# First feed-forward product of a hybrid encoder layer: one of four weight sums a pair added by the transfer from DRAM, and the low part of one weight block formed by a rounding transfer within SBUF

## The chip, the cores and the metric

The kernel runs on one core of one Trainium2 chip. The metric is device time in microseconds (us) for one execution of the whole layer; lower is better. Of the kernel before, three runs were timed, and one more execution was recorded by the hardware profiler. An engine is named as in the profile: PE multiplies matrices, PEld loads its weights, DVE and ACT are the vector and scalar engines, POOL is GpSimd, SP issues DMA transfers.

## The reference

One layer of an encoder on 1024 tokens of width 1024: two attention groups, a cross-attention into 256 memory tokens, and a feed-forward block of hidden width 4096, each with a norm before and after. The part that matters here is the last one:

```python
h = rmsnorm(x, g_ff_pre[l])
y = jnp.square(jax.nn.relu(h @ w_ff1[l])) @ w_ff2[l]
x = x + rmsnorm(y, g_ff_post[l])
```

All values are float32.

## The kernel before, in words

**Numbers in two parts.** A float32 operand of a product is split into a high part (the value rounded to the type fp32r, by a copy on ACT) and a low part (the value less its high part, on DVE or POOL). `mm3` (lines 172 to 176) multiplies high by high, high by low and low by high: three matmuls of 128x128 by 128x512.

**The first feed-forward product.** `w_ff1` is cut into 32 column blocks of 128 columns, each loaded as one tile of 128 partitions by 1024 (512 KB). They are taken in 16 pairs (block j and block j + 16), and the tokens in two halves, so that one pair is a 2x2 block product. It is done in Strassen's way with seven products instead of eight, each of 12 matmuls: with the left half of the weights' features called k0 and the right half k1, a pair needs the block sums that `Weights.sums` and `Weights.sum4` (lines 1799 to 1811) make from the two raw tiles r0 and r1:

- line 1802: sc[k1] = r0[k0] - r1[k0]
- line 1803: r1[k0] = r1[k0] + r1[k1], in place, so that r1 becomes the block "s1a"
- line 1804: sc[k0] = r1[k0] - r0[k0]; sc is the block "s23"
- line 1809: sd = r0[k1] - sc[k0], the block "s4"

Each is a 128x512 operation. Pair 0 has them on DVE, ahead of the loop (`cur.sums(nc.vector)`), and pairs 1 to 15 on POOL. `Weights.split` (lines 1813 to 1820) then splits the blocks: high part on ACT (line 1597), low part on DVE (line 1600).

**The loop over pairs.** Instructions are written out by hand, and each engine runs its own in that order. In the pass of pair j stand, in this order: the sums of pair j + 1; the load of r0 of pair j + 2; from pair 7 on the two products with block "a" (`first_row`; for pairs 0 to 6 these were made before the loop and kept in DRAM, and `reload` brings them back as tile p1r, line 1841); the product of s23 with T2 into bank x; u2 = x + p1 (line 1943); the stores of the pair before (`sums()`); the product of s1a with T1 into bank z; the splits of "a" (from pair 7 on) and s23 of pair j + 1; the product of s23 with T3, added into bank x, so that it waits for the reading of x at line 1943; u3 (line 1958 on DVE for pairs 0 to 6, line 1960 on ACT after that) and g22 = z + u3 (line 1962); the load of r1 of pair j + 2; the reload of p1r of pair j + 1; the product of s1a with T4 into bank v; the split of s1a of pair j + 1; the product of s4 with B22, added into bank z, so that it waits for line 1962. So a pass is five products for pairs 0 to 6 and seven for pairs 7 to 15.

**Buffers.** Raw weight tiles rotate through three buffers of tag wraw; only r1 of pair 1 (`wfu`, line 1794) is taken from the pool u4. High and low parts of "a" and "s1a" rotate through two buffers each. The pool u4 (lines 153 to 155) holds tiles of 4 KB a partition for the whole kernel: tokens in two parts, queries and keys, some weights, x, p1r. A tile gets a buffer at its first write, and that write waits until an earlier tile of the buffer has been used for the last time. All transfers are issued by SP, in order.

**The plan of the attention phase.** From line 459 on, a planner in Python orders the instructions of the attention phase with costs and tokens; it counts six free u4 buffers at its start and gives and takes such tokens. `Outputs.pump` (lines 878 to 886) starts the first group of output loads (lines 920 to 929) once 12 tokens are free.

**Scratch for descriptors.** Line 2184 builds the program with a scratch space of 256 bytes a partition for transfers that POOL issues; the kernel before issues none.

Of the kernel before, what the change touches and what calls it, by code (L numbers as in the profile page):

```python
# [17 lines left out]
AF = mybir.ActivationFunctionType  # L18
ALU = mybir.AluOpType
# [116 lines left out]
def build(ctx, tc, nc, out, t):  # L136
    def pool(name, bufs=1, space=None, stack=ctx, **kw):
        if space is not None:
            kw["space"] = space
        return stack.enter_context(tc.tile_pool(name=name, bufs=bufs, reuse_waits="tile", **kw))  # L140
# [4 lines left out]
    up = pool("u4")  # L145
# [6 lines left out]

    def u4(name, shape, dt=F32R):

        return up.tile(list(shape), dt, tag="u4", bufs=34, name=name)

    class Act:


        def __init__(self, name, n=HT):  # L160
            self.per = 1024 // n
            m = KC // self.per
            self.h = [u4(f"{name}_hi{i}", (P, self.per, n)) for i in range(m)]
            self.l = [u4(f"{name}_lo{i}", (P, self.per, n)) for i in range(m)]
# [35 lines left out]
    od = [[[dr.tile([P, HT], F32, name=f"od{k}_{h}{m}") for m in "hl"] for h in range(2)] for k in range(KC)]  # L200
# [18 lines left out]
    def bias_rows(part):  # L219

        if part == 0:
# [13 lines left out]
    free = {k: Tokens(flow, n) for k, n in  # L235
            dict(s=2, tr=2, pv=2, mm=2, sp=5, p=2, klo=4, bias=2, raw=2, w=2, ot=3, u4=6,
                 q=4, mp=4, pt=1, xt=2, wq=0).items()}
    seen = {}

    def there(*keys):  # L240
        return all(flow.past(seen.get(k, math.inf)) for k in keys)
# [11 lines left out]
    class Stock:  # L253
# [48 lines left out]
        def hi(self, key):  # L302
            raw, nm = self.raw[key], "_".join(map(str, key))
            home, shape = self.home.get(key, "w"), list(raw.shape)
            if home == "w":
                w = [wp.tile(shape, F32R, tag=x, bufs=2, name=x + nm) for x in ("whi", "wlo")]
            elif home == "wq":
                w = [p2x.tile(shape, F32R, tag="wq", bufs=2, name=x + nm) for x in ("whi", "wlo")]
            else:
                w = [u4(x + nm, shape) for x in ("whi", "wlo")]  # L310
            nc.scalar.activation(w[0], raw, AF.Copy)
            self.w[key] = w
# [243 lines left out]
    def turn_steps():  # L556
        for n, a, g in units:
            for c, (kbs, slots, dead) in enumerate(key_steps(n, g)):
                yield (0.109 * (4 - len(dead)),
                       lambda: there(("p", n, a, g, 0), ("p", n, a, g, 1)) and free["tr"].ready() and free["p"].ready())  # L560
                free["tr"].take()
                free["p"].take()
                nm = f"{n}{a}{g}{c}"
                live = slice(1 if dead == [0] else 0, 3 if dead == [3] else 4)
                whole = mark(("t", n, a, g, c))
                tr = mm_tile([P, 4, P], f"ptr{nm}", "tr")
                ph = p1.tile([P, 4, P], F32R, tag="ph", bufs=2, name=f"ph{nm}")
                pl = p1.tile([P, 4, P], F32R, tag="pl", bufs=2, name=f"pl{nm}")
                for m, (j, q) in enumerate(slots):
                    if m not in dead:  # L570
                        sp, b0, i = probs[n, a, g][q]
                        k = kbs[j] - b0
                        nc.tensor.transpose(tr[:, m, :], sp[:, k * P:(k + 1) * P], ident)  # L573

                def split(at, ph=ph, pl=pl, tr=tr, live=live, whole=whole):
                    def done(end):
                        whole(end)
                        free["tr"].give(end)
                    flow.put("V", at, 0.56 if dead else 0.7, lambda: nc.vector.tensor_sub(pl[:, live, :], tr[:, live, :],  # L579
                                                                        f(ph[:, live, :])), done)  # L580

                flow.put("S", flow.end, 0.49 if dead else 0.6, lambda ph=ph, tr=tr, live=live: nc.scalar.activation(  # L582
                    ph[:, live, :], tr[:, live, :], AF.Copy), split)
                trs[n, a, g, c] = ph, pl
            for _ in range(1 + (g > 1)):
                free["sp"].give(flow.end)
# [285 lines left out]
    class Outputs:  # L872
# [5 lines left out]
        def pump(self):  # L878
            while self.left:
                th, g = self.left[0]  # L880
                if not (there(("od", g)) and ((th, g) == (0, 0) or there("keys")) and free["u4"].ready(12 if (th, g) == (0, 0) else 9)):
                    break
                self.left.pop(0)
                for _ in range(9):
                    free["u4"].take()
                self.one(th, g)

        def one(self, th, g):
# [21 lines left out]
            for i in range(2):  # L910
                for j in range(2):
                    kc = g * 4 + i * 2 + j
                    gc, o, dh, dl = gcol[:, kc:kc + 1], os[i][:, j, :], yh[i][:, j, :], yl[i][:, j, :]
                    dst = sq if kc % 4 == 0 else o

                    low = ol[i][:, j, :]

                    def loaded(at, gc=gc, o=o, dh=dh, dl=dl, dst=dst, low=low, last=i == 1 and j == 1):
                        flow.chain(at, [
                            (eng, add_cost, lambda: adder.tensor_add(o, o, low)),  # L920
                            ("S", 0.63, lambda: nc.scalar.activation(dh, o, AF.Copy, scale=gc)),
                            ("V", 0.75, lambda: nc.vector.scalar_tensor_tensor(
                                dl, o, gc, f(dh), op0=ALU.mult, op1=ALU.subtract))],
                            lambda end: (split(end), flow.put("S", end, 0.63, lambda: nc.scalar.activation(
                                dst, o, AF.Square), squared, 1)), 1)

                    here = all_of(("oin", th, kc), 2, loaded)
                    for m, x in enumerate((o, low)):
                        flow.load(flow.now, lambda x=x, kc=kc, m=m: nc.sync.dma_start(x, od[kc][th][m]), here, 3.0)
# [619 lines left out]
    NP = FF // (2 * P)  # L1549
# [117 lines left out]
    class Turn:  # L1667
# [26 lines left out]
        def sums(self):  # L1694
            a, i = self.a, self.i
            b12, b22 = self.src
            c12, d2 = t2(f"c12_{a}{i}"), t2(f"T2_{a}{i}")
            nc.scalar.activation(c12, b12, AF.Copy)
            d1, d4 = xf[i, a], xf[i + 2, a]
            nc.vector.tensor_sub(d1, b12, d1)  # L1700
            lo22 = self.hi("B22", b22)
            nc.vector.tensor_sub(d2, b22, d1)
            lo2 = self.hi("T2", d2)
            nc.vector.tensor_sub(c12, b22, c12)
            lo1 = self.hi("T1", d1)
            lo22()
            nc.vector.tensor_sub(d4, d2, d4)
            lo3 = self.hi("T3", c12)
            lo4 = self.hi("T4", d4)
            self.los = [lo2, lo1, lo3, lo4]  # L1710
# [71 lines left out]
    k0, k1 = slice(0, HT), slice(HT, D)  # L1782

    class Weights:
# [14 lines left out]
        def sums(self, eng=nc.gpsimd):  # L1799
            j, (r0, r1) = self.j, (self.raw[0], self.raw[1])  # L1800
            sc = pw.tile([P, D], F32, tag="sc", bufs=1, name=f"sc{j}")
            eng.tensor_sub(sc[:, k1], r0[:, k0], r1[:, k0])  # L1802
            eng.tensor_add(r1[:, k0], r1[:, k0], r1[:, k1])
            eng.tensor_sub(sc[:, k0], r1[:, k0], r0[:, k0])
            self.src = {"a": (r0, D, wp, "w"), "s23": (sc, D, pws, "v"), "s1a": (r1, D, wp, "w")}

# [5 lines left out]
        def split(self, n):  # L1812
            raw, width, p, tag = self.src[n]
            if p is pws:
                q = self.j % 2
                self.w[n] = HiLo(raw, width, pws[q], f"{tag}{q}", 1, f"{n}{self.j}").both(nc.vector)
            else:
                self.w[n] = HiLo(raw, width, p, tag, 2, f"{n}{self.j}").both(nc.vector)

    cur, nxt = Weights(0), Weights(1)  # L1820
    cur.load(0)
# [99 lines left out]
    with manual:  # L1921
        sums = lambda: None
        for j in range(NP):
# [20 lines left out]
            else:  # L1944
                nc.scalar.activation(u2, x, AF.Copy)
            sums()
            relu2(g11)
            put(j, 0, g11)
# [50 lines left out]

            cur, nxt = nxt, after  # L2000
        sums()


# [184 lines left out]
```

## Time and profile before

| what | value |
|---|---|
| median of three runs | 1492.26 us (1491.24 to 1492.3) |
| the profiled execution's own time | 1491.91 us |
| its span, first to last instruction | 1490.1 us |
| PE busy | 1466.0 us, 98% |
| DVE, ACT, POOL busy | 928.4, 795.2, 375.7 us |
| loop over pairs 0 to 15 | about 909 to 1170 us of the span |
| granted TensorE clock | 0.997 |

The span leaves out 1.81 us around the instructions. Busy time of PE counts matmuls that overlap, so a share near 100% says that PE had something in it, not that it ran at its peak. A line number in the profile is that of the kernel's text; where a helper issues an instruction (1597, 1600, 174 to 176), the tile's name tells which block it is.

### The profile page before, as it was taken

To read this page: it belongs to the slowest core of one execution; us is meant where nothing else is said; L and a number is where in the kernel's file an instruction comes from. 1 tells how busy PE (TensorE), PEld (TensorE's weight loads), DVE (VectorE), ACT (ScalarE), POOL (GpSimd) and SP (SyncE) were. 2 spreads that over 40 slices of the span, in tenths; PEclk is the share of its full clock that TensorE was granted. 3 is DMA by queue.
4 is the path that set the end of the run, shared out by engine and by line. 5 is a ranking of instruction groups with operands and counts; after the bars stand their busy time and mean duration, and the time that the engine had idled before them with its cause. 6 is when DMAs were issued, how large, how long until landed. Compare 5 with 4: busy or idle time off the path is not lost. (4 is left out here: it accounts for less than half of the span.)

```text
span 1490.1 us, 21429 instructions
## 1 busy us (share of the span) xinstructions
PE 1466.0 (98%) x7564; PEld 1249.1 (84%) x7564; DVE 928.4 (62%) x1599; ACT 795.2 (53%) x1426; POOL 375.7 (25%) x464
## 2 busy tenths in 40 slices
PE   8899999999999999999999999999999999999998
PEld 7788888888889987888888887888888888888886
DVE  4857666566465654884374587675555665646577
ACT  6647666666566663554363455555555553443442
POOL 1324354344343310431031423432333000000021
PEclk9999999999999999999999999999999999999999
DMA  8033323524225568461251355764445685436475
GB/s 326 29 87 107 86 67 79 168 79 133 77 75 155 175 234 313 156 212 57 85 170 57 126 171 201 265 233 155 149 157 175 234 344 191 141 129 209 173 252 198
DMA packets 95355, 239.54 MB, mean 161 GB/s; under 512 B 11896, under 2 KB 20224, under 8 KB 95248
## 3 DMA queue, kind: packets, MB, share of 16 engines
q1 hardware_dynamic: 95248, 238.18, 47.8%
q8 instruction: 59, 0.97, 0.3%
q14 instruction: 48, 0.39, 0.1%
HBM read 170.45 MB, written 59.30 MB: 154 GB/s over the span
## 5 line engine op out<-in xcount | busy, mean ns | idle before, releaser
L579 DVE TENSOR_TENSOR pl<-ptr,ph 128x512 fp32r<-128x512 f32 (+1 forms) x152 | 92.3, 616 | 63.2 <-ACT ph L582 62.6
L582 ACT ACTIVATE ph<-ptr 128x512 fp32r<-128x512 f32 (+1 forms) x152 | 79.6, 539 | 48.7 <-PE ptr L573 45.4
L1912 ACT ACTIVATE whif<-ra 128x1024 fp32r<-128x1024 f32 x37 | 39.2, 1060 | 122.6 <-PE fy L175 62.6
L1914 DVE TENSOR_TENSOR wlof<-ra,whif 128x1024 fp32r<-128x1024 f32 x37 | 45.3, 1225 | 91.4 <-ACT whif L1912 91.3
L2028 POOL TENSOR_SCALAR rf<-sf 128x1 f32<-128x1 f32 x8 | 7.4, 928 | 326.4 <-ACT jf L2013 326.1
L174 PE MATMUL fx<-vhif,whif 128*128 128x512 f32 x168 | 65.4, 390 | 0.0
L176 PE MATMUL fx<-vhif,wlof 128*128 128x512 f32 x168 | 65.4, 389 | 0.0
L175 PE MATMUL fx<-vlof,whif 128*128 128x512 f32 x168 | 65.4, 389 | 0.0
L613 PE MATMUL pv<-pl,vs 128*128 128x256 f32 (+1 forms) x304 | 64.6, 294 | 0.2 <-DVE pl L579 0.2
L613 PEld LDWEIGHTS pv<-ph,vs 128*128 128x128 f32 x304 | 53.2, 189 | 7.3
L613 PE MATMUL pv<-ph,vs 128*128 128x256 f32 (+1 forms) x304 | 58.1, 273 | 0.0
L1802 POOL TENSOR_TENSOR sc<-wf,wf 128x512 f32<-128x512 f32 x14 | 21.2, 1513 | 142.3 <-DMA wf<-in_w_ff 121.3
L174 PE MATMUL k<-hT_hi,whik 128*128 128x512 f32 x128 | 52.9, 413 | 0.0
L174 PE MATMUL mq<-h2T_hi,whimq 128*128 128x512 f32 x128 | 51.7, 404 | 0.0
L174 PE MATMUL yw<-whiwo,yT_hi 128*128 128x512 f32 x128 | 50.9, 398 | 0.7 <-ACT yt L1065 0.7
L174 PE MATMUL q<-hT_hi,whiq 128*128 128x512 f32 x128 | 51.0, 398 | 0.0
L175 PE MATMUL k<-hT_lo,whik 128*128 128x512 f32 x128 | 50.5, 395 | 0.0
L174 PE MATMUL ym<-whimo,oT_hi 128*128 128x512 f32 x128 | 50.4, 395 | 0.1
L176 PE MATMUL k<-hT_hi,wlok 128*128 128x512 f32 x128 | 50.4, 394 | 0.0
L175 PE MATMUL q<-hT_lo,whiq 128*128 128x512 f32 x128 | 50.2, 392 | 0.0
L175 PE MATMUL mq<-h2T_lo,whimq 128*128 128x512 f32 x128 | 50.1, 391 | 0.0
L176 PE MATMUL q<-hT_hi,wloq 128*128 128x512 f32 x128 | 50.1, 391 | 0.0
(597 smaller groups left out, 4989.4 us busy)
## 6 DMA issues: line engine op xcount, KB each, us to landing
ra<-gd SPq DMA_DIRECT2D x56, 512.0 KB, 3.9
wg<-in_w_ff SPq DMA_DIRECT2D x56, 512.0 KB, 5.1
wf<-in_w_ff SPq DMA_DIRECT2D x38, 512.0 KB, 3.8
gd<-s SPq DMA_DIRECT2D x48, 256.0 KB, 2.1
wrawmq<-in_w_mq SPq DMA_DIRECT2D x16, 512.0 KB, 4.1
wrawmo<-in_w_mo SPq DMA_DIRECT2D x16, 512.0 KB, 3.8
gd<-u SPq DMA_DIRECT2D x32, 256.0 KB, 2.1
gd<-g SPq DMA_DIRECT2D x25, 256.0 KB, 2.9
```

The lines of the kernel that those rows point to most:

```text
L174: nc.tensor.matmul(ps, lh, rh, start=start, stop=False, skip_group_check=more)
L175: nc.tensor.matmul(ps, lh, rl, start=False, stop=False, skip_group_check=more)
L176: nc.tensor.matmul(ps, ll, rh, start=False, stop=stop, skip_group_check=more)
L579: flow.put("V", at, 0.56 if dead else 0.7, lambda: nc.vector.tensor_sub(pl[:, live, :], tr[:, live, :], f(ph[:, live, :])), done)
L582: flow.put("S", flow.end, 0.49 if dead else 0.6, lambda ph=ph, tr=tr, live=live: nc.scalar.activation(ph[:, live, :], tr[:, live, :], AF.C ...
L613: nc.tensor.matmul(pv[:, q0:q0 + k1 - k0, :], v, x[:, k0:k1, :], start=c == 0 and m == 0, stop=c + 1 == len(steps) and m == 3, skip_group_ ...
L1802: eng.tensor_sub(sc[:, k1], r0[:, k0], r1[:, k0])
L1912: nc.scalar.activation(ah, ra, AF.Copy)
L1914: nc.vector.tensor_sub(al, ra, f(ah))
L2028: nc.gpsimd.tensor_scalar(r, ssf[b][:, 0:1], ssf[b][:, 1:2], EPS, op0=ALU.add, op1=ALU.add)
```

## The change

Four things are changed.

1. In `sums`, line 1803 is no longer an addition. POOL issues a transfer that reads the right half of block j + 16 from DRAM a second time and adds it to r1[k0] in SBUF. That holds for all 16 pairs, pair 0 among them, whose other sums stay on DVE.
2. In `split`, the low part of s1a of pairs 1 to 15 is no longer a subtraction on DVE. ACT writes the negated block, rounded to fp32r, into the low tile; then POOL issues a transfer within SBUF that adds the raw block to it.
3. The program is built with the default scratch space for descriptors in place of 256 bytes, and the pool u4 has 30 buffers in place of 34.
4. The first group of output loads in the attention phase starts at 11 free tokens in place of 12. The planner's count of free buffers at its start stays at six.

```diff
-        return up.tile(list(shape), dt, tag="u4", bufs=34, name=name)
+        return up.tile(list(shape), dt, tag="u4", bufs=30, name=name)
...
-                if not (there(("od", g)) and ((th, g) == (0, 0) or there("keys")) and free["u4"].ready(12 if (th, g) == (0, 0) else 9)):
+                if not (there(("od", g)) and ((th, g) == (0, 0) or there("keys")) and free["u4"].ready(11 if (th, g) == (0, 0) else 9)):
...
             eng.tensor_sub(sc[:, k1], r0[:, k0], r1[:, k0])
-            eng.tensor_add(r1[:, k0], r1[:, k0], r1[:, k1])
+            nc.gpsimd.dma_start(r1[:, k0], t['w_ff1'][j + NP].rearrange('p a b -> p (a b)')[:, k1], accum_op=ALU.add)
             eng.tensor_sub(sc[:, k0], r1[:, k0], r0[:, k0])
...
-                self.w[n] = HiLo(raw, width, p, tag, 2, f"{n}{self.j}").both(nc.vector)
+                h = self.w[n] = HiLo(raw, width, p, tag, 2, f"{n}{self.j}")
+                if n == "s1a" and self.j:
+                    h.split_hi()
+                    nc.scalar.activation(h.lo, raw, AF.Copy, scale=-1.0)
+                    nc.gpsimd.dma_start(h.lo, raw, accum_op=ALU.add)
+                else:
+                    h.both(nc.vector)
...
-    nc = bacc.Bacc("TRN2", target_bir_lowering=False, num_devices=1, dynamic_dma_scratch_size=256)
+    nc = bacc.Bacc("TRN2", target_bir_lowering=False, num_devices=1)
```

## The prediction

> **What bounds the kernel now.** I read the page's first part for the span, then busy time in windows, and last the timelines, engine by engine, around the places that the change touches.
>
> ```profile
> span 1490.1 us, 21429 instructions
> PE 1466.0 (98%) x7564; PEld 1249.1 (84%) x7564; DVE 928.4 (62%) x1599; ACT 795.2 (53%) x1426; POOL 375.7 (25%) x464
> ```
>
> ```profile
> 325.00:350.00 25.00, 25.00 (x156) 22.26 (x155) 11.44 (x31) 13.90 (x29) 8.32 (x10) 1.00 0.40 129
> ...
> 475.00:600.00 125.00, 123.37 (x696) 107.10 (x695) 74.90 (x147) 72.50 (x133) 24.89 (x27) 1.00 0.68 232
> ...
> 900.00:907.00 7.00, 6.33 (x28) 4.92 (x27) 5.25 (x9) 3.72 (x6) 0.00 (x0) 1.00 0.32 85
> 907.00:921.00 14.00, 12.97 (x58) 10.33 (x56) 8.95 (x12) 5.11 (x7) 5.15 (x4) 1.00 0.98 342
> ...
> 948.00:962.00 14.00, 14.00 (x63) 11.61 (x62) 10.08 (x13) 7.76 (x13) 5.18 (x4) 1.00 0.76 262
> 1003.00:1100.00 97.00, 97.00 (x430) 80.34 (x429) 50.13 (x61) 51.70 (x78) 29.26 (x21) 1.00 0.44 149
> ```
>
> A row of the windows has the stretch and its length, then busy us of PE, PEld, DVE, ACT and POOL, the granted clock, the share of the transfer engines' time and GB/s. In the two rows from 948 to 1100 PE is busy in every microsecond, while DVE, which the change relieves, has 50.13 of 97 and POOL 29.26: taking work from either shortens nothing there. PE's idle time in the loop lies in 907 to 921: 14.00 less 12.97, 1.0 us. That is all there is to gain in the loop; the question is which new waits reach PE.
>
> **The two durations that no row shows.** X is the time from a POOL-issued adding transfer of 256 KB from DRAM to its landing, Y that of the 512 KB transfer within SBUF. The nearest rows (KB each, median us from issue to landing):
>
> ```profile
> wf<-in_w_ff SPq DMA_DIRECT2D x38, 512.0 KB, 3.8
> gd<-s SPq DMA_DIRECT2D x48, 256.0 KB, 2.1
> x<-in_x SPq DMA_DIRECT2D x8, 512.0 KB, 9.7
> x1d<-xtw SPq DMA_DIRECT2D x8, 512.0 KB, 2.6
> p1r<-p1d SPq DMA_DIRECT2D x7, 512.0 KB, 5.6
> ```
>
> X lies between 2.1 (a plain store) and 9.7 (the crowded start), Y between 2.6 and 9.7. An adding transfer must read its target too and passes through POOL, so I take more than a plain load: X = 4 where the transfer engines are a third busy (before 907), 5 for both X and Y where they are full. The Trainium skill (DMA: Bandwidth & Descriptors, Anatomy of one DMA, SWDGE path) fits 2.0 us plus bytes over 436 GB/s for a transfer that POOL issues; by it, as an estimate, X is 2.6 and Y 3.2, the terms below come to 4.7 us in place of 10.4, and no row here can show it, since the kernel before has no such transfer.
>
> **Pair 0's sums (change 1).** These are ahead of the loop on DVE:
>
> ```profile
> 904.38 0.69 DVE L1803 TENSOR_TENSOR wf<-wf 128x512 f32<-128x512 f32 x1
> 905.11 0.69 DVE L1804 TENSOR_TENSOR sc<-wf,wf 128x512 f32<-128x512 f32 x1
> ...
> 906.93 1.23 DVE L1600 TENSOR_TENSOR v0lo_s<-sc,v0hi_s 128x1024 fp32r<-128x1024 f32 x1 [0.40 <-ACT v0hi_s L1597]
> ...
> 909.38 0.39 PE L176 MATMUL px<-T_hi,v0lo_s 128*128 128x512 f32 x1
> ...
> 914.81 0.69 DVE L1943 TENSOR_TENSOR u<-px,p1r 128x512 f32<-128x512 f32 x1 [1.92 <-DMA p1r<-p1d]
> ...
> 915.56 0.50 PE L174 MATMUL px<-T_hi,v0hi_s 128*128 128x512 f32 x1 [1.03 <-DVE u L1943]
> ```
>
> (A row of a timeline has start and length in us, engine and line, the tiles written and read, and in brackets the idle time before it with what ended it.)
>
> Line 1803 starts at 904.38, when line 1802 is done. In its place the transfer is issued, and line 1804 waits on DVE for its landing: 904.4 + 4 = 908.4 in place of 905.11. Queued behind it on DVE are sd, the low part of s23 and the low parts of T1 and T3; ACT waits for sc. Line 1804 ends at 909.1, the high part (1.06 for 128x1024, as in the next fence) at 910.2, the low part (1.23) at 911.4. PE's first low product of the loop starts at 909.38 in the trace, so it comes 2.1 late. The 1.03 us that PE then waited at 915.56 for u2, and u2 for p1r, is swallowed by that, so the product with T3 of pair 0 starts 1.1 late. The removed addition gives back 0.69 and costs 4.
>
> **Pairs 0 and 1 (changes 1, 2 and 3).**
>
> ```profile
> 914.83 1.28 POOL L1803 TENSOR_TENSOR wfu<-wfu 128x512 f32<-128x512 f32 x1
> ...
> 917.50 1.06 ACT L1597 ACTIVATE v1hi_s<-sc 128x1024 fp32r<-128x1024 f32 x1 [1.47 <-POOL sc L1804]
> ...
> 918.60 1.33 DVE L1600 TENSOR_TENSOR v1lo_s<-sc,v1hi_s 128x1024 fp32r<-128x1024 f32 x1 [3.09 <-ACT v1hi_s L1597]
> 919.85 0.68 DVE L1958 TENSOR_TENSOR u<-px,p1r 128x512 f32<-128x512 f32 x1
> 920.56 0.69 DVE L1962 TENSOR_TENSOR g<-pz,u 128x512 f32<-128x512 f32 x1
> ...
> 921.40 0.47 PE L174 MATMUL pz<-B_hi,u0hi_s 128*128 128x512 f32 x1
> ...
> 916.91 0.46 SPq L1841 DMA_DIRECT2D p1r<-p1d  x1
> ...
> 929.65 0.39 PE L174 MATMUL px<-T_hi,v1hi_s 128*128 128x512 f32 x1
> ```
>
> These rows are one chain already: POOL's third sum, ACT, DVE, and behind DVE's split, in order, u3 and g22, for which PE's B22 product waits. With the transfer the third sum runs from 914.8 + 5 = 919.8 to 921.1; high part to 922.1, low part to 923.4, u3 to 924.1, g22 to 924.8, and B22 starts at 924.9 in place of 921.4: 3.5 late.
>
> Then the buffers. When `reload` brings p1r of pair 1, the pool u4 holds 28 tiles of the tokens (8 for B11 and B21, 20 for the five blocks T1 to T4 and B22), `wfu`, p1r of pair 0 and this one: 31. With 34 buffers SP issued it at 916.91; with 30 it waits for the last use of `wfu`, which is now the rounding transfer of s1a of pair 1. ACT reaches that block at 922.1 (high part to 923.2, negated copy to 924.2), and with Y = 5 it lands at 929.2. SP issues the reload at 929.3, 5.6 more to 934.9, u2 0.7, and PE's T3 product of pair 1 starts at 935.7 in place of 929.65: **6.1 late** in all, the 3.5 and 1.1 within it. Stores of g22 and u3 and the next r0 stand behind the reload on SP; their readers come later than that. T1 of pair 1 needs the low part only at 930.9.
>
> **Pairs 2 to 6.** Rows of pair 2:
>
> ```profile
> 946.92 0.69 DVE L1962 TENSOR_TENSOR g<-pz,u 128x512 f32<-128x512 f32 x1
> ...
> 948.69 0.39 PE L174 MATMUL pz<-B_hi,u0hi_s 128*128 128x512 f32 x1
> ...
> 950.38 1.29 POOL L1802 TENSOR_TENSOR sc<-wf,wf 128x512 f32<-128x512 f32 x1 [7.12 <-DVE u1lo_s L1600]
> ```
>
> g22 ends at 947.61, 1.1 ahead of B22. A cycle closes here: first sum 2.8 after g22 (950.38), 1.3, X, third sum 1.3, then 3.7 for ACT's high part, DVE's low part, u3 and g22: 9.1 + X against a pass of 13.6. It decides at X = 4.5; at X = 5 each of five passes loses 0.5, less the 1.1 of slack: 1.4. The low part of s1a follows the third sum by 3.2 (ACT's two high parts and the negated copy) + Y, and PE reads it 9.6 after that sum (3.7, then B22 and T2 of 2.7 each, and 0.5): covered up to Y = 6.4. POOL waits for the negated copy with the next pair's first sum behind it, but that sum comes 6.5 after the third, later than the copy. **1.4**.
>
> **Pairs 7 to 15.** A pass is 19 us, and the covers are long:
>
> ```profile
> 1061.94 1.72 POOL L1802 TENSOR_TENSOR sc<-wf,wf 128x512 f32<-128x512 f32 x1 [12.88 <-DMA wf<-in_w_ff]
> ...
> 1060.18 1.06 ACT L1597 ACTIVATE whi_s1a<-wf 128x1024 fp32r<-128x1024 f32 x1 [1.89 <-PE pv L175]
> 1075.11 1.04 ACT L1597 ACTIVATE v1hi_s<-sc 128x1024 fp32r<-128x1024 f32 x1
> ...
> 1071.54 0.39 PE L176 MATMUL pz<-T_hi,wlo_s1a 128*128 128x512 f32 x1
> ...
> 1064.87 0.38 SPq L1585 DMA_DIRECT2D wf<-in_w_ff  x1
> ...
> 1073.82 0.32 SPq L1621 DMA_DIRECT2D gd<-s  x1
> ```
>
> The third sum must be done by 1075.1; from 1061.9 that leaves 10.6 us for X less POOL's wait for ACT's negated copy. That copy ends at 1062.2 and the low part is read at 1071.5, so Y may take 9.2. ACT's extra 1.05 falls into its idle time. The raw buffer is held until the landing, past 1064.87 where SP refilled it before; SP's next transfer stands at 1073.82. **0**, and beyond 9 us the wait is PE's.
>
> **The early buffers (change 3).** At the first projections u4 holds 16 tiles of tokens, 8 of values, 4 of weights and 2 of queries: 30. The two key tiles make 32.
>
> ```profile
> 79.89 1.21 ACT L709 ACTIVATE kd<-k 64x512 fp32r<-64x512 f32 x2 [3.40 <-PE k L176]
> ...
> 81.13 1.41 DVE L710 TENSOR_TENSOR kl<-k,kd 64x512 fp32r<-64x512 f32 x2 [1.08 <-ACT kd L709]
> ...
> 84.91 0.39 PE L176 MATMUL q<-hT_hi,wloq 128*128 128x512 f32 x1
> 85.13 0.39 PE L174 MATMUL k<-hT_hi,whik 128*128 128x512 f32 x1
> ```
>
> ACT's write of the keys must wait for a buffer, the first to come free being the query weights, last read at 84.91 + 0.39. Then 1.2 on ACT and 1.4 on DVE, to 88.0, before PE may write the same PSUM bank (two of that tag, and the other is just filled). PE started at 85.13: **2.9**. SP's copies of the keys and the bias loads behind them move by 5 us, and the first scores by 2.9 with PE.
>
> **Change 4** starts a group of loads and adds earlier at about 342 us, where PE is busy 25.00 of 25.00. Without a row of that order I take 0, between -2 (the stretch 475 to 600 has 125.00 less 123.37, 1.6 us, of idle PE) and +5 (four POOL additions of 1.3 in front of POOL's softmax work).
>
> **Sum.** 6.1 + 1.4 + 2.9 = 10.4. The span 1490.1 becomes 1500.5, the profiled execution 1491.91 (1.81 outside the span) 1502.3; the median of the runs, 1492.26, is 0.35 above that execution: **1502.7**.
>
> **Rivals.** *The transfers are slower, or the transfer engines fill up.* In 948 to 962 they are 0.76 busy at 262 GB/s, so full at 345. A pair adds 0.79 MB: 2.3 us of their time if moved once, 4.6 if the target is read as well, and 3.3 of 13.6 are free. The second count would overflow by 1.3 us a pass, and loads, reloads and stores would be late together. The Trainium skill (DMA: Bandwidth & Descriptors, Queues, rings and completion order) has each transfer engine take turns packet by packet between queues, so that a queue of POOL's own would bring no engines of its own; the share of 0.98 in pair 0 is where it would show first. With X = Y = 7: pairs 0 and 1 lose 10.0 by the same chain (the reload at 933.3), five passes 2.5 for X and 0.6 for the low part, less 1.1: 2.9 + 10.0 + 14.4 = 27, **1519**. It decides from X = 4.5 on.
>
> *No slower.* The buffers decide: if the framework finds the key tiles and p1r buffers whose last use is over, 2.9 and the reload's wait fall away, and only B22's wait in pair 0 stays, X - 1.5; below X = 4.5 that is under 3 us: **1493 to 1495**. Against it speaks the count of live tiles.
>
> *Faster.* Change 4 alone can do it, by filling PE's gaps after 475; it would have to bring over 6 us, and the gaps of that stretch are 1.6.
>
> *The forecast with quick transfers*, X = 2.6 and Y = 3.2: **1497**.
>
> **How the numbers follow.** Forecast with its quick variant, 1496 to 1509: 0.57. Slower transfers, 1509 to 1530: 0.28. No slower: 0.12. Faster: 0.03. A measurement tells 0.2% (3 us) from no change, so slower by more holds 0.85, within 0.12, faster 0.03. The range runs from 1494 to 1522: it leaves out the faster case, about half of the one with no change and the upper quarter of the slow one, some 0.16.
>
> **What would show it.** ACT's first key write at about 85.4; the reload of pair 1 on SP at about 929; g22 and B22 of pair 0 at 925; POOL's third sum 5 us after its transfer's issue; PE full from pair 7 on. Wrong would be PE stalls in pairs 7 to 15 (X or Y beyond 9), or a pass of pairs 2 to 6 well over 13.6.

## The result and the profile after

The changed kernel takes 1515.39 us in the median of four runs (1509.43, 1513.63, 1517.14, 1517.68), beside 1491.76 for the kernel before, timed with it: 1.0157 times as long, with a 95% interval of 1.0141 to 1.0173, so 23.6 us slower. The profiled execution is the quickest of the four (1509.43), so its trace shows 17.6 us of the 23.6 in its span.

First the page after the change: span and busy time, the transfer queues, the issues.

```profile
span 1507.7 us, 21486 instructions
...
PE 1469.6 (97%) x7564; PEld 1248.3 (83%) x7564; DVE 912.7 (61%) x1583; ACT 809.3 (54%) x1441; POOL 380.9 (25%) x480
...
q1 hardware_dynamic: 95248, 238.18, 46.2%
q0 software_dynamic: 4464, 12.06, 4.4%
...
wf<-in_w_ff SPq DMA_DIRECT2D x38, 512.0 KB, 4.7
gd<-s SPq DMA_DIRECT2D x48, 256.0 KB, 2.9
...
wlo_s1a<-wf POOLq DMA_DIRECT2D x14, 512.0 KB, 4.7
```

DVE is 16 us less busy, as the change meant it to be, and that shortens nothing. Queue q0 is new: 12.06 MB that keep all 16 transfer engines for 4.4% of 1507.7, 66 us. SP's queue moves 238.18 MB in 46.2%, 697 us. POOL's queue takes 5.5 us a MB, SP's 2.9. Loads of 512 KB land after 4.7 us in place of 3.8.

Next, what PE waits for from 900 us to 1200 us after the change (total, times, longest):

```profile
PE px L174 <- ACT v0hi_s L1597: 5.4, 1, 5.4
PE pz L176 <- DMA wlo_s1a<-wf: 5.3, 4, 1.6
PE pz L174 <- DVE g L1968: 1.3, 3, 0.7
PE px L174 <- DVE u L1949: 1.1, 1, 1.1
PE px L176 <- DVE wlo_a L1600: 0.8, 1, 0.8
```

Three of these are new: the high part of s23 of pair 0 (the run-in), four low parts of s1a (the rounding transfer), and g22. The fourth, u2 behind the reload, has moved from pair 0 to pair 1. They come to 13.1 us, 1.0 of which was there before, while the kernel falls 17.8 us behind from the start of the loop to its end (table below). Much of the rest is the clock, as the windows show (PE, PEld, DVE, ACT, POOL busy, granted clock, transfer share, GB/s; a packet counts in the window in which it starts, so a share can pass 1):

```profile
82.90:87.00 4.10, 4.06 (x11) 3.23 (x12) 1.30 (x2) 0.00 (x0) 0.00 (x0) 0.61 0.88 202
...
908.00:913.00 5.00, 0.49 (x3) 0.07 (x1) 0.95 (x2) 0.26 (x1) 0.00 (x0) 1.00 1.03 303
913.00:920.00 7.00, 6.11 (x14) 4.33 (x15) 6.60 (x8) 3.90 (x6) 2.55 (x2) 0.52 0.32 82
942.00:1010.00 68.00, 62.98 (x272) 50.18 (x270) 34.94 (x49) 38.80 (x58) 25.68 (x23) 1.00 0.95 280
1020.00:1187.00 167.00, 166.51 (x734) 137.17 (x733) 76.30 (x94) 94.22 (x141) 46.91 (x41) 1.00 0.64 186
```

From 913 to 920 PE is busy, but with 14 matmuls in 7 us, at a granted clock of 0.52. From 942 to 1010 (most of pairs 2 to 6) PE lacks 5.0 of 68 us, and the transfer engines are at 0.95. From pair 7 on PE is all but full: 166.51 of 167 us.

Matching PE's matmuls one by one between the two timelines gives the balance:

| matmul | before | after | later by |
|---|---|---|---|
| a key product just ahead of the new wait | 75.05 | 70.14 | -4.9 |
| first product of the second key tile | 85.13 | 82.94 | -2.2 |
| scores, some 15 us on | 100.13 | 99.81 | -0.3 |
| last products ahead of the loop | 900.22 | 899.49 | -0.7 |
| T2 of pair 0, first matmul | 908.93 | 913.85 | +4.9 |
| T3 of pair 0 | 915.56 | 922.56 | +7.0 |
| T3 of pair 1 | 929.65 | 937.43 | +7.8 |
| T1 of pair 2, first low part | 940.98 | 950.72 | +9.7 |
| the same of pair 5 | 981.78 | 996.00 | +14.2 |
| the same of pair 6 | 995.38 | 1011.26 | +15.9 |
| in pair 7 | 1025.07 | 1041.17 | +16.1 |
| second product, fx | 1200.09 | 1217.21 | +17.1 |

This execution began 4.9 us ahead by chance (the same product stands between 4.8 us earlier and 0.4 later in the traces of the other kernels, and no run here shows why). Counted from there, the change costs 4.6 at the keys, -0.4 in the attention, 8.5 up to T3 of pair 1, 8.3 in pairs 2 to 6, 1.0 in pairs 7 to 15: 22.0, near the median's 23.6.

**The run-in.** Timelines of POOL, DVE and PE after the change:

```profile
904.38 1.08 POOL L1803 DMA_DIRECT2D wf<-in_w_ff  x1 [27.50 <-DVE sc L1802]
...
912.01 0.69 DVE L1804 TENSOR_TENSOR sc<-wf,wf 128x512 f32<-128x512 f32 x1 [8.27 <-DMA wf<-in_w_ff]
...
913.85 0.80 PE L174 MATMUL px<-T_hi,v0hi_s 128*128 128x512 f32 x1 [5.36 <-ACT v0hi_s L1597]
```

Issued at 904.38, the adding transfer releases line 1804 at 912.01: 7.6 us. It stands beside everything SP issues from 903 to 909 (share 1.03 from 908 to 913).

**A pass of pairs 2 to 6.** POOL's timeline after the change, then SP's, over one pass:

```profile
987.73 0.89 POOL L1822 DMA_DIRECT2D wlo_s1a<-wf  x1 [1.92 <-ACT wlo_s1a L1821]
991.87 1.28 POOL L1802 TENSOR_TENSOR sc<-wf,wf 128x512 f32<-128x512 f32 x1 [3.25 <-DMA wf<-in_w_ff]
993.45 0.89 POOL L1803 DMA_DIRECT2D wf<-in_w_ff  x1 [0.30 <-POOL sc L1802]
998.18 1.28 POOL L1804 TENSOR_TENSOR sc<-wf,wf 128x512 f32<-128x512 f32 x1 [3.84 <-DMA wf<-in_w_ff]
999.54 1.30 POOL L1809 TENSOR_TENSOR sd<-wf,sc 128x512 f32<-128x512 f32 x1
```

```profile
985.84 0.33 SPq L1585 DMA_DIRECT2D wf<-in_w_ff  x1
986.22 0.42 SPq L1847 DMA_DIRECT2D p1r<-p1d  x1
...
996.01 0.33 SPq L1585 DMA_DIRECT2D wf<-in_w_ff  x1
...
1000.86 0.33 SPq L1585 DMA_DIRECT2D wf<-in_w_ff  x1
```

The round closes without PE: load of r1 (985.84) to first sum 6.0, first sum 1.3, gap 0.3, adding transfer 4.7, two sums 2.7, and at 1000.86, when the fourth sum has freed r0's buffer, the next load of r1: 15.0 us against a pass of 13.6. (From pair 2 to pair 6 the passes take 14.7 to 15.4.) The rounding transfer (issued at 987.73) is in flight beside that load; PE's product with the low part starts 8.3 us later, at 996.00. The row at 996.01 shows something else: SP's load of the next r0 starts when the rounding transfer has landed, for that transfer still holds the raw buffer.

### The profile page after: what moved, and what is told of

Same layout as the page of the kernel before. It is cut to its first block, busy times and chain, and to the rows that moved or that the text cites. A ratio compares the mean times of both kernels' runs of the same rounds, so it can differ in the third digit from the quotient of the medians.

```text
span 1507.7 us, 21486 instructions
## 1 busy us (share of the span) xinstructions
PE 1469.6 (97%) x7564; PEld 1248.3 (83%) x7564; DVE 912.7 (61%) x1583; ACT 809.3 (54%) x1441; POOL 380.9 (25%) x480
## 3 DMA queue, kind: packets, MB, share of 16 engines
q1 hardware_dynamic: 95248, 238.18, 46.2%
q0 software_dynamic: 4464, 12.06, 4.4%
## 5 line engine op out<-in xcount | busy, mean ns | idle before, releaser
L176 PE MATMUL mq<-h2T_hi,wlomq 128*128 128x512 f32 x128 | 50.0, 390 | 0.0
```

What stands on the lines that cost most here:

```text
L176: nc.tensor.matmul(ps, ll, rh, start=False, stop=stop, skip_group_check=more)
```

## The experiments

Each was timed beside runs of the kernel before, whose median stands in brackets. "With all fixes" below means pair 0's addition on DVE, 33 buffers in u4, 704 bytes of scratch space, four raw weight buffers, and r1 loaded right behind r0. In the code, `...` stands for what is left out.

### The buffers alone

```diff
-        return up.tile(list(shape), dt, tag="u4", bufs=34, name=name)
+        return up.tile(list(shape), dt, tag="u4", bufs=30, name=name)
...
-... free["u4"].ready(12 if (th, g) == (0, 0) else 9)):
+... free["u4"].ready(11 if (th, g) == (0, 0) else 9)):
...
-    nc = bacc.Bacc("TRN2", target_bir_lowering=False, num_devices=1, dynamic_dma_scratch_size=256)
+    nc = bacc.Bacc("TRN2", target_bir_lowering=False, num_devices=1)
```

> Changes 3 and 4 alone: 30 buffers, the default scratch space, the start at 11 tokens; no transfer by POOL. The forecast's term: PE waits 2.9 us at the second key tile, and nothing in the feed-forward product, so 1491.8 + 2.9 = 1494.7. Rival: in the trace after the change PE's second key product waited 2.7 us, but PE stood 0.3 us ahead of the kernel before at 100 us of the span, so an early start of the projections may swallow the wait: 1491.5. A second rival is the reload of pair 1, which has one buffer too few here as well, but whose buffer comes free with DVE's low part at about 920: reload landing at 926, no wait at 929.65.

Measured: 1495.33 (1491.07), ratio 1.0028 [1.0017, 1.0040]: 4.3 us. The wait is there (2.7), neither swallowed nor alone: the matmuls behind it run at half the pace and lose 1.8 more. In the trace of the whole change that is the granted clock of 0.61 from 82.90 to 87.00. The second rival costs nothing: T3 of pair 1 is no later than the products ahead of the loop (3.4 us behind the kernel before, against 3.5).

### Pair 0's addition back on DVE

```diff
+            if j:
                 nc.gpsimd.dma_start(r1[:, k0], ..., accum_op=ALU.add)
+            else:
+                eng.tensor_add(r1[:, k0], r1[:, k0], r1[:, k1])
```

> The changed kernel with pair 0's addition back on DVE. After the change PE waited 5.4 us for pair 0's high part, ran at a granted clock of 0.52 from 913 to 920, and was 7 us late there. Theory 1, the losses add up: without that transfer 7 us come back, 1508.4. Theory 2, they lie beside each other: POOL's first sum of pair 1 was only 1.65 us later than before (915.15 against 913.5), and from it follow the rounding transfer of pair 1, the reload at 930.46 and the raw buffers of the next pairs, so PE meets the same lateness at T3 of pair 1, and only about 1.7 us come back: 1513.7. In the trace PE would then wait some 6 us more in pair 1 (for p1r), and no slow clock would stand at 913 to 920 unless a wait of that length comes first.

Measured: 1521.14 (1491.07), ratio 1.0190 [1.0168, 1.0212]. Not quicker at all: theory 1 falls, and theory 2 is right that the losses lie beside each other, but gives back too much: up to T3 of pair 1 the trace loses 9.0 us in place of 8.5, and pairs 2 to 6 lose 11.0 in place of 8.3. PE's waits from 895 us on and the timeline at pair 0's B22:

```profile
PE pz L174 <- DVE g L1971: 7.8, 4, 6.1
PE pz L176 <- DMA wlo_s1a<-wf: 5.9, 3, 2.2
```

```profile
934.48 0.76 PE L174 MATMUL pz<-B_hi,u0hi_s 128*128 128x512 f32 x1 [6.14 <-DVE g L1971]
935.04 0.63 PE L175 MATMUL pz<-B_lo,u0hi_s 128*128 128x512 f32 x1
935.47 0.63 PE L176 MATMUL pz<-B_hi,u0lo_s 128*128 128x512 f32 x1
```

The wait that the run-in had hidden, g22 behind the third sum of pair 1, is now 6.1 us, and the half clock (0.43 from start to start in place of 0.23) follows that one.

### One transfer at a time

Buffers, scratch space and start as in the change. Adding alone (`e_acc`):

```diff
-                if n == "s1a" and self.j:
+                if False:
```

Rounding alone (`e_lo`):

```diff
-            nc.gpsimd.dma_start(r1[:, k0], ..., accum_op=ALU.add)
+            eng.tensor_add(r1[:, k0], r1[:, k0], r1[:, k1])
```

> The adding transfers alone (change 1 with 3 and 4); the low part of s1a is a subtraction on DVE again. Passes 2 to 6 took 15.0 us after the change in place of 13.6. Theory R, the raw buffers: the fourth sum frees a buffer, the load takes 6.0, first sum 1.6, transfer 4.7, two more sums 2.6, in all 15.0; that round has no rounding transfer in it, so the passes stay at 14 to 15 us, and only the reload of pair 1 comes earlier (its buffer is free at about 925 in place of 930.4): 1515.4 - 4 = 1511. Theory Y, the rounding transfer (8 us from issue to PE's read where 6.4 are covered) sets the passes: they go back to 13.6 to 14.1, and it is 1515.4 - 4 - 6 = 1505.

> The rounding transfers alone (change 2 with 3 and 4); the sum r1[k0] + r1[k1] is an addition again, on DVE for pair 0 and on POOL after that. Theory R: the round through the raw buffers is 11.5 us without the transfer, under 13.6, so passes 2 to 6 lose nothing; the reload of pair 1 waits for the rounding transfer of wfu, 3 us late at T3 of pair 1, and the keys cost 2.8: 1491.8 + 6 = 1498. Theory Y: the rounding transfer still takes 8 us where the forecast counted 6.4 of cover, 1.4 a pass: 1505.

Measured: adding alone 1507.49 (1491.07), ratio 1.0103 [1.0079, 1.0127]; rounding alone 1510.36, ratio 1.0125 [1.0104, 1.0146]. Neither theory holds for both runs. With adding alone pairs 2 to 6 lost 5.3 us by the matched matmuls, with passes of about 14.5: that is inside R's 14 to 15 and over Y's 14.1, though the whole came out 3.5 us under R's 1511. With rounding alone, to which R gave some 3 us in the loop and Y some 10, the loop lost 12.8. Its PE waits:

```profile
PE pz L174 <- DVE g L1968: 5.1, 4, 2.1
PE pz L176 <- DMA wlo_s1a<-wf: 2.7, 1, 2.7
PE px L174 <- DVE u L1949: 2.2, 3, 1.3
```

g22 is late though its sums hold no transfer. POOL's first sum waits for the load of r1 (8.1 us of idle POOL at 993.59, for a load issued at 985.81).

### Is it SP's order?

```diff
-            if after:
-                after.load(0)
-            elif more:
+            if not after and more:
                 fetch(0)
...
             if after:
+                after.load(0)
                 after.load(1)
```

> The rounding transfers alone, as in the run before, with one line moved: in each pass the load of r0 of pair j + 2 is issued after the five stores, directly ahead of the load of r1. Theory H (held buffer): the raw buffer of r1 stays taken until the rounding transfer lands (10.5 us after its issue in the pass at 940), SP waits there for it with the five stores, the load of r1 and the reload behind it, and these then come in one burst, in which the load of r1 takes 6 to 8 us. With the line moved SP waits for nothing, passes 2 to 6 go back to about 13.6, and some 9 of the 18.8 us over the kernel before come back: 1501. Theory V (volume): the transfer engines are too full whatever the order; 1510 stays.

> The whole change, with the load of r0 of pair j + 2 moved behind the five stores. Theory H: what is left in passes 2 to 6 is the round of the sums with the adding transfer (0.5 to 1 a pass in the run with adding transfers alone), so 3 to 5 us come back: 1511. Theory V: 1515 stays.

Measured: 1517.08 (1492.56), ratio 1.0164 [1.0148, 1.0180], and 1523.19, ratio 1.0205 [1.0176, 1.0234]. Both are slower than without the move, so the gain that theory H forecast did not come. That alone does not refute H, since the move brings something new: in the run with rounding alone two loads, the reload and the rounding transfer are now issued within 2 us of each other (988.20 to 989.77), and the first sum starts at 997.18, 7.9 us after the later load (989.31). It suggests that what counts is what lies beside the load of r1. The fourth raw buffer, further down, tests H without the crowding.

### 34 buffers again, and the late pairs alone

```diff
-        return up.tile(list(shape), dt, tag="u4", bufs=30, name=name)
+        return up.tile(list(shape), dt, tag="u4", bufs=34, name=name)
...
-    nc = bacc.Bacc("TRN2", target_bir_lowering=False, num_devices=1)
+    nc = bacc.Bacc("TRN2", target_bir_lowering=False, num_devices=1, dynamic_dma_scratch_size=704)
```

and, for the late pairs (`e_late`, 30 buffers):

```diff
+            if j >= AHEAD:
                 nc.gpsimd.dma_start(r1[:, k0], ..., accum_op=ALU.add)
+            else:
+                eng.tensor_add(r1[:, k0], r1[:, k0], r1[:, k1])
...
-                if n == "s1a" and self.j:
+                if n == "s1a" and self.j >= AHEAD:
```

> The whole change with 34 buffers in u4 again, and 704 bytes of scratch space. The wait at the second key tile goes (2.7 us, and 1.9 more that PE lost at the slower clock behind it), and the reload of pair 1 finds a buffer (1.3 us on top of the run-in's lateness). If these add up: 1515.4 - 6 = 1509.5. Rival: a small scratch space makes POOL wait for descriptors before it can issue, which would show as longer issues of the transfers, and the gain is smaller.

> Both transfers in pairs 7 to 15 only; pairs 0 to 6 have additions and subtractions again; 30 buffers, default scratch. The forecast gave this part 0: then the time is that of the buffers alone, 1495.3. In the trace after the change PE lost 1.1 us at B22 of pairs 8 to 15, which would make it 1496.4. Rival: what held these pairs together was the lateness of the earlier ones, and they cost more by themselves: 1498 or over.

Measured: 1511.41 (1492.56), ratio 1.0131 [1.0107, 1.0154]: 18.9 us over the kernel before in place of 23.6, so 4.7 of the 6 came back by the medians, though the interval overlaps that of the whole change. In the trace the 6 are back where they were expected (3.7 us at the keys, 2.6 up to T3 of pair 1), and pairs 2 to 6 lose 2.6 more. POOL's issues of the rounding transfer took 0.90 us, and 0.89 with the large scratch space, so the rival falls. And 1498.16 (1492.56), ratio 1.0040 [1.0024, 1.0055], where the buffers alone had 1.0028: 1.8 us more, with intervals that overlap. Pairs 7 to 15 may not be quite free.

### Away from the load of r1

`e_lo_raw4` has four raw buffers (at every tile of tag wraw; one is shown); `e_lo_raw4e` also moves the load of r1 ahead. `e_lo_copy` is the three-buffer kernel with `accum_op` left out of the rounding transfer, so it does not compute the layer and serves for its time alone:

```diff
-        raw = wp.tile([P, D], F32, tag="wraw", bufs=3, name=name)
+        raw = wp.tile([P, D], F32, tag="wraw", bufs=4, name=name)
...
             if after:
                 after.load(0)
+                after.load(1)
...
-            if after:
-                after.load(1)
-            elif not more:
+            if not after and not more:
```

> The rounding transfers alone (the run at 1510.4) with four raw weight buffers in place of three and 1024 bytes of scratch space; the order is as in the change. Theory H (held buffer): the load of r0 of pair j + 2 finds a buffer at once, nothing queues behind it on SP, passes 2 to 6 go back to 13.6: 1501. Theory C (collision): the load of r1 and the reload of p1r still stand within 1 to 2 us of the rounding transfer, which takes 2.8 us of all 16 transfer engines by the queue's row (2.8% of 1508.3 us for 15 transfers); the load of r1 keeps its 7 to 8 us in place of 4.2, and the time stays at 1508 to 1510.

> As the run with four raw buffers, and the load of r1 of pair j + 2 issued right behind that of r0, at the start of the pass, half a pass ahead of the rounding transfer. Theory C: POOL's first sum no longer waits for a load that lies beside the rounding transfer, passes 2 to 6 go back to 13.6, what stays is the keys' 4.6 and 3 to 6 us at pairs 1 and 2: 1501. Theory H: no more gain than four buffers alone.

> The rounding transfers alone, as plain copies: the same bytes, queue, place and waits, but the transfer overwrites the low part in place of adding to it (so the low part of s1a is the rounded block, not the remainder). If reading the target is what fills the transfer engines, a transfer takes 1.5 us of them in place of 2.8, lands 1 to 3 us sooner, and a good part of the loss in passes 2 to 6 goes: 1503 to 1506. Rival: the price is that of a transfer issued by POOL, whatever it does: 1510.

> The whole change with every wait named so far taken away: pair 0's addition on DVE, u4 with 33 buffers and 704 bytes of scratch space (no wait at the keys, a buffer for the reload), four raw buffers, r1 loaded right behind r0. What stays if these are the causes: B22 of pair 0 (6.0 us in the run with pair 0 on DVE, and 2 more behind it), now perhaps 4, and 0.5 a pass from the round of the sums with the adding transfer: 1491.8 + 6 = 1498. Rival: the transfer engines, 4.4 us a pair against 3.3 free, are what binds passes 2 to 6: 1503 to 1508.

Measured, beside 1490.25: four buffers alone 1507.61, ratio 1.0109 [1.0092, 1.0126], little gained (the interval overlaps that with three); with the early load 1495.49, ratio 1.0033 [1.0021, 1.0045], what the 30 buffers alone cost and 5.5 us quicker than theory C's 1501, since pairs 1 and 2 lost nothing either; as plain copies 1500.87, ratio 1.0064 [1.0047, 1.0082], so 9 of the 19 us gone, more than expected, with 1.6 us of all engines a transfer in place of 2.8 and a landing after 2.9 us in place of 4.7 (medians over all pairs); the whole change with all fixes 1498.70, ratio 1.0051 [1.0034, 1.0068]. For the rounding transfer theory C holds and H falls. The windows of rounding alone, without and with the early load:

```profile
942.00:1010.00 68.00, 61.52 (x259) 49.07 (x258) 41.42 (x47) 36.54 (x54) 27.36 (x21) 0.97 0.83 255
```

```profile
942.00:1010.00 68.00, 67.95 (x300) 55.92 (x299) 38.80 (x55) 40.65 (x58) 25.66 (x23) 1.00 0.87 276
```

PE goes from 61.5 to 67.95 of 68 us with more transferred, not less. So the rounding transfer alone fits into the engines; it hurt by standing beside the one load on whose landing the next pair's sums wait. That the whole change with all fixes met its 1498 is in part luck: pair 0's B22, for which 4 us were forecast, lost nothing. Where the time went stands in the next section.

### Volume or place

`e_acc_raw4e` and `e_lo_best` are one transfer each with all fixes (the edits above, put together; the output loads start at 12 tokens, while the runs with both transfers keep 11), `e_ctl` has four raw buffers, 33 buffers in u4 and the new order without a transfer, `e_late_acc` the adding transfer in pairs 7 to 15 alone with 34 buffers. `e_fix_copy` is the whole change with all fixes and the edit below; as it leaves out both additions, it too serves for its time alone:

```diff
-                nc.gpsimd.dma_start(r1[:, k0], ..., accum_op=ALU.add)
+                nc.gpsimd.dma_start(r1[:, k0], ...)
...
-                    nc.gpsimd.dma_start(h.lo, raw, accum_op=ALU.add)
+                    nc.gpsimd.dma_start(h.lo, raw)
```

> The adding transfers alone in pairs 1 to 15 (pair 0 on DVE), with 33 buffers, 704 bytes of scratch space, four raw buffers, r1 loaded right behind r0, start at 12 tokens. The run with both transfers and the same order took 1498.7. Place: the transfer's 5 us stand in the round first sum, transfer, third sum, high part, low part, u3, g22, and that is the whole loss, 0.5 to 1 us a pass: 1498 again. Volume: without the rounding transfers (2.8 us of all transfer engines a pair) there is room, and it is 1493 to 1494.

> The rounding transfers alone, with 33 buffers, 704 bytes of scratch space, four raw buffers, r1 loaded right behind r0, start at 12 tokens. In the run with 30 buffers this took 1495.5, as much as the 30 buffers alone (1495.3); with the buffers back the 4 us of the keys go as well: 1491.3, no different from the kernel before. Rival: some of the 1495.5 was the transfers' own: 1493.

> The kernel before with four raw buffers in place of three, 33 in u4 and r1 loaded right behind r0; no transfer by POOL. PE waits 1.0 us in the loop before, at 915 for the reload, so at most 1 us is to gain: 1490.5 to 1491.5. If the order by itself gains more than that, the runs with this order have to be read against it and not against the kernel before.

> The adding transfers alone, in pairs 7 to 15 alone, with 34 buffers and 704 bytes of scratch space, start at 12 tokens. Both transfers in these pairs with 30 buffers took 1498.2, the buffers alone 1495.3. If the adding transfer is what costs there (it moves POOL's third and fourth sum by 5 us, beside DVE's four sums of the pair before, which then take 1.6 us in place of 0.7): 1491.5 + 2.5 = 1494. If the rounding transfer costs it: 1491.5.

> The run with both transfers and every wait removed (1498.7), with both transfers as plain copies: the same bytes, queue, places and waits, but they overwrite their targets in place of adding to them (so s1a and its low part are not the sums). Each transfer alone cost nothing in that order, both together 7 us. Volume: what fills the transfer engines is the reading of the target, 4.4 us a pair in place of 2.4; as copies they fit, and it is 1492 to 1493. Place and queue: two transfers issued by POOL in one pass are what costs, whatever they do, and 1498 stays.

Measured: adding alone 1492.86 (1491.56), ratio 1.0007 [0.9996, 1.0018]; rounding alone 1493.44, 1.0008 [0.9997, 1.0018]; no transfer 1492.05, 0.9996 [0.9987, 1.0006]; adding in the late pairs 1494.74, 1.0018 [1.0009, 1.0027]; both as copies 1491.20 (1491.85), 0.9996 [0.9987, 1.0005]. Each alone is free within what can be told, both together cost 7.6 us by the ratio, and both as plain copies are free again. So the price is that of adding, as the volume theory has it, and neither the queue's nor the number of transfers. The queue's row on the page and the window, of both with adding and then of both as copies, and last the window of the kernel before:

```profile
q0 software_dynamic: 4320, 11.80, 4.5%
```

```profile
942.00:1010.00 68.00, 65.47 (x283) 52.28 (x282) 41.97 (x53) 40.11 (x57) 29.93 (x25) 1.00 0.90 282
```

```profile
q0 software_dynamic: 3360, 11.80, 2.5%
```

```profile
942.00:1010.00 68.00, 67.90 (x299) 55.75 (x298) 46.61 (x56) 40.85 (x58) 26.96 (x25) 1.00 0.86 293
```

```profile
942.00:1010.00 68.00, 68.00 (x302) 56.34 (x301) 49.42 (x60) 35.67 (x53) 28.14 (x21) 1.00 0.69 236
```

The same 11.80 MB cost 4.5% of 1498.0 us, 4.5 us of all transfer engines a pair, as sums, and 2.5% of 1492.7, 2.5 a pair, as copies. Before the change these 68 us had a share of 0.69, so 4.2 us of a 13.6 us pass were free. By the Trainium skill (Collectives: The Full Stack, The bandwidth ceiling) a reduce-scatter between cores runs at half the rate of a plain gather because its add needs two source reads, not because adding takes time, with a measured ratio of 1.93; the ratio here, for transfers within one core, is 1.8.

That the engines overflow is not shown, though, and it is not where most of the loss lies. By the matched matmuls the run with all fixes loses 8.9 us from T3 of pair 1 on: 3.1 up to T1 of pair 6, 1.3 more at B22 of pair 6, and 4.4 in pairs 7 to 15, where the share was 0.50 before and is 0.65 (1020 to 1187). As copies the three are 0.3 each at most. In the loop its PE waits for g22 alone, and two of DVE's four sums (1020 to 1190) take 1.2 and 1.1 us in the mean in place of 0.7:

```profile
PE pz L174 <- DVE g L1972: 5.2, 7, 1.3
```

```profile
L1999 DVE TENSOR_TENSOR s<-u,g 128x512 f32<-128x512 f32 x8 | 9.3, 1160 | 30.3 <-ACT u L1618 30.3
L2001 DVE TENSOR_TENSOR u<-g,u 128x512 f32<-128x512 f32 x8 | 8.5, 1060 | 0.3
```

In pairs 7 to 15 the adding transfer lands 6.5 to 7.6 us after its issue here, 3.7 to 4.2 when it is alone and 3.4 to 6.0 as a copy. In this trace POOL's third and fourth sums come so late that they run beside DVE's four sums, and g22 and PE's B22 come after those. That fits two transfers that have room on the mean and hurt by landing later beside each other; no run takes it apart further.

In the late pairs the rows of `e_late_acc` show what the adding transfer does there. It moves POOL's sums into DVE's splits:

```profile
994.24 1.83 POOL L1807 TENSOR_TENSOR sc<-wf,wf 128x512 f32<-128x512 f32 x1 [4.16 <-DVE s L2004]
...
994.83 2.32 DVE L1600 TENSOR_TENSOR wlo_a<-wf,whi_a 128x1024 fp32r<-128x1024 f32 x1
...
996.15 2.15 POOL L1812 TENSOR_TENSOR sd<-wf,sc 128x512 f32<-128x512 f32 x1
...
997.20 2.18 DVE L1600 TENSOR_TENSOR v1lo_s<-sc,v1hi_s 128x1024 fp32r<-128x1024 f32 x1
...
1000.86 0.47 PE L174 MATMUL pz<-B_hi,u0hi_s 128*128 128x512 f32 x1 [1.16 <-DVE g L1971]
```

Two splits of 1.22 us take 2.32 and 2.18 beside POOL's sums, and PE waits 1.2 us in the pass of pair 6. By the matched matmuls that is 1.3 us of the 2.7 that the ratio gives; for the rest I found no row, and it stays open. The expectation had put the slow stretch at DVE's four sums, which took 0.77, 0.69, 0.68 and 0.69 us in the mean from 1020 to 1190: the kind of wait was right, its place not. (With all fixes, above, it is those sums.)

No version beats the kernel before. The order without a transfer, where at most 1 us was to gain, comes out the same.

## Why the prediction was wrong

The direction was right, but 10.4 us were forecast and 23.6 came. The time lies in the range only because the range made room for the rival with slower transfers.

**The step that failed: pairs 2 to 6, 1.4 us.** It took X = 5 and Y = 5 as properties of one transfer, put them into a round (9.1 + X against 13.6) and a cover (Y up to 6.4), and left the volume to the rival. Measured are 8.3 us. X was about right: the adding transfer takes 3.7 to 6.7 us in the loop, 5.4 in the median. Y was not: the rounding transfer lands after 6.0 to 9.5 us in these pairs, and PE waits for it in four of the five. And the round was another one. The step let POOL's first sum follow g22 by 2.8 us, from a row (950.38) in which DVE released it. In the passes around that one it waits for the load of r1, already in the kernel before:

```profile
963.66 1.29 POOL L1802 TENSOR_TENSOR sc<-wf,wf 128x512 f32<-128x512 f32 x1 [7.86 <-DMA wf<-in_w_ff]
```

After the change that load cannot start before the fourth sum has freed its buffer, and from issue to first sum it takes 5.5 to 6.4 us in the passes of pairs 4 to 6, beside the rounding transfer, in place of 4.0 to 4.9. With all fixes the 8.3, between the same two matmuls, become 4.6, and as plain copies 0.7: about half went with the place, buffers included, and about half with the adding.

The rival was nearer in kind: it counted 4.6 us of all engines a pair "if the target is read as well", and the queue's rows say 4.3 to 4.5. It was given a chance of 0.28, and its price was worked out from X = Y = 7 and not from that count. That its overflow of 1.3 us a pass is close to the 1.5 by which the passes grew is luck: over 942 to 1010 the free time was 4.2 us and not 3.3, and with all fixes 4.5 us of transfers cost 0.7 a pass. What no step had: even a volume that fits hurts by its place. Rounding alone lost 12.8 us in the loop with 0.83 of the engines busy from 942 to 1010, and nothing with 0.87 once r1 was loaded early.

**The clock behind a wait had no term.** The key tiles were forecast at 2.9, with ACT's write at 85.3 and PE at 88.0; in the run with pair 0 on DVE, which started nearly as the kernel before did, they stood at 85.30 and 88.09. But the matmuls behind the wait ran at half pace: with them it is 4.3 us by the run of the buffers alone. In the run-in the slow stretch took 3.3 us.

**Pairs 0 and 1, 6.1 us**: 8.5 measured. In it X = 4 was wrong for the run-in. It was chosen from a share of 0.32 ahead of 907, but the transfer was in flight from 904 to 912, where the row quoted for 907 to 921 had 0.98; it took 7.6. The loop's first low product came 6.5 us late, counted from the loop's start, in place of 2.1, of which 5.4 are PE's wait for the high part. That cost little in the end, since the chain to the reload was late anyway: SP issued it at 930.46 (forecast 929.3), T3 of pair 1 stood at 937.43 (935.7). The losses lay beside each other, as the step had it; taking pair 0's transfer away gained nothing.

**Pairs 7 to 15, 0 us**: 1.0 measured, with PE busy 166.5 of 167 us. The step set POOL's sums against ACT's high part alone and had no term for DVE: where its splits or sums run beside POOL's late sums they are slower. That cost 1.3 us in the run with adding in the late pairs alone, and the 4.4 us with all fixes may be the same. **Change 4, 0 us**: fits, as the attention moved by -0.4; no run has change 4 alone.

## What to carry to other kernels

Price a transfer that adds at nearly twice its bytes and set it against the free share of the transfer engines in that stage, for the whole group of transfers at once: two that are free one by one may not be together. Room on the mean is not enough: ask what each transfer stands beside, since the load on whose landing the next round waits should be issued early enough not to meet it, and a later landing can move one engine's work beside another's. And a new wait of PE of 2 us or more can be charged twice, once as itself and once as a slow stretch behind it.

## What the hardware showed that was not expected

The granted clock falls after short waits. A wait of 2.67 us at the keys was followed by a stretch that lost 1.9 us by the matched matmuls, one of 5.36 by 3.3, one of 6.14 by 2.3, and one of 2.1 (rounding alone, B22 of pair 5) by 1.5. Over the traces of all 19 kernels, from 48 us of the span on, none of 42 waits of PE between 1.0 and 1.93 us was followed by a lower granted clock within 5 us, 16 of 25 between 2.00 and 2.67 were, and all 23 from 2.91 up. So between 2.0 and 2.7 the length alone does not decide: of two waits of 2.67 us in the run with rounding alone, the one at the keys was followed by a slow stretch and the one in pair 2 was not. The Trainium skill (TensorE: Matmul & The Clock Gate, HAM oscillation — how this bites in real kernels) has the rule that gaps over about 3.4 us throttle PE; here gaps from 2.0 us on could do it and all from 2.91 did, so the measurement decides for the shorter bound.
